# Retention's queries, keys and values as products of 512 columns in a hybrid decoder trunk

## The chip, the core and the metric

The kernel runs on one core of a Trainium2 chip. Its time is the device time of one execution in microseconds (us). Five engines work side by side, each in the order of its own queue: TensorE (PE, with its weight loads as PEld), VectorE (DVE), ScalarE (ACT), GpSimd (POOL) and SyncE (SP, which here issues DMAs). They wait for each other at semaphores. Matrix products accumulate in PSUM banks of 128 x 512 fp32; everything else lies in SBUF, 128 partitions wide.

## The reference, cut to what matters

Two layers (DEPTH = 2), a sequence of 1024 tokens, width 1024, all in fp32. Each layer has three groups of heads that read one projection of the normalised input: sliding-window attention (a), retention (r) and gated linear attention (g).

```python
h = rms_norm(x, pre_gain) * (1.0 + scale) + shift
proj = h @ w_in
(aq, ak, av, ag, rq, rk, rv, rg, gq, gk, gv, gg, ga) = jnp.split(proj, IN_SPLITS, axis=-1)
...
rq = apply_rotary(rq.reshape(B, S, RET_HEADS, RET_DK), positions, ret_freq)
rk = apply_rotary(rk.reshape(B, S, RET_HEADS, RET_DK), positions, ret_freq)
r = retention(rq, rk, rv.reshape(B, S, RET_HEADS, RET_DV))
r_out = rms_norm(r).reshape(B, S, RET_W) * jax.nn.silu(rg)
...
y = jnp.concatenate([a_out, r_out, g_out], axis=-1) @ w_out
return x + gate * rms_norm(y, post_gain)
```

Rotation turns the two halves x1, x2 (32 columns each) of every head's 64 columns into x1 cos - x2 sin and x2 cos + x1 sin. Retention runs over 8 chunks of 128 tokens with 4 heads of 64 columns: in each chunk the masked scores of queries against keys times the values, plus the queries times a state that is carried on from chunk to chunk; the state is a sum of decayed key-value products:

```python
sc = jnp.einsum('bhid,bhjd->bhij', qi, ki) * dmask
intra = jnp.einsum('bhij,bhjv->bhiv', sc, vi)
inter = jnp.einsum('bhid,bhdv->bhiv', qi * q_decay, state)
new_state = chunk_decay * state + jnp.einsum('bhjd,bhjv->bhdv', ki * k_decay, vi)
```

Queries, keys, values and retention's gate rg are 256 columns each of w_in; so are gg (the gate of the g group, with 16 columns more) and the other units.

## The kernel before

**Tiles and products.** The sequence is cut into 8 tiles t of 128 tokens, 4 pairs p of tiles, 2 halves hf of 4 tiles. Every fp32 operand is held as a high and a low part. A product over the 1024 inner columns is three passes (high x high, low x high, high x low) over 8 blocks k of 128: 24 matmuls that accumulate in one bank (`accum`). `project` holds the tile's 128 tokens (h) as the stationary side and moves the weights, 256 columns; its result has tokens on partitions. `project_P` and `project_T` hold 128 columns of the weights and move the tokens: a pair's 256, or a half's 512 from two tiles of memory with `both`; the result is transposed, with head columns on partitions. There are three banks for such products (the names `mm`) and five for the small ones (`aux`).

**Retention before.** For each pair p: `ret_q` makes two products of 24 matmuls of 256 columns into the two halves of one bank, and VectorE turns them: four operations 32 x 512, which read one quarter of the partitions of the bank, multiply with the sine and write to the neighbouring quarter (two of them with a factor -1), one product with the cosine, one sum. Then follow the keys of two tiles and the values of two tiles, 24 matmuls of 256 columns each, each in a bank of its own. A key tile is rotated by `rotary` on VectorE (five operations); a value tile is scaled by one. `ret_core` is the step of a tile: two transposes of the rotated keys on TensorE, a copy to SBUF by ScalarE, the scores (TensorE), two masks (VectorE), the outputs and the state's update (TensorE), the state's sum and decay (VectorE), then the norm and the gate (`head_norm_gate`: square by ScalarE, sum by VectorE, power by POOL, two products by VectorE, transposes).

**Order of the work.** TensorE's order is written out by hand, through a model clock. Each `mult` moves the clock on; `job` hands in a generator such as `ret_core`, whose `yield` says how long the model waits until the next piece of it may be issued (the table `L` holds these numbers; `rc1` is the wait before the key transposes, a name with @1 holds for layer 1); `flag` and `await_flag` do the same for results that others wait for. `pump` is called after each few matmuls and issues all pieces that are due in between. For the other engines a scheduler sets the order.

**Weights.** They are loaded in units of 1024 x 256 by `load`: four DMAs of 256 KB on SP into staging buffers, then converted to high and low parts by VectorE, ScalarE and POOL into one of seven places (`PLACES`; 0 to 2 lie in one array, `arena_71` in the orders below, 3 to 6 in another, `arena_479`). A place is free when the products of the unit that it held are done. `PLACE` says which unit goes where (the number `_w` is 0 in layer 0 and 2 in layer 1). Before: rg 5, rq 6, rk `_w`, rv 5; rv therefore follows rg in the same place, and its load is called behind the last gate product. SP also carries the stores of finished gates (srS, sgS), of the sine tables (tabA), and the loads of modulation weights (ms).

## Time and profile before

| | us |
|---|---|
| median of 3 runs (lowest, highest) | 981.45 (981.32, 981.62) |
| profiled execution, its own time | 980.64 |
| its span, first to last instruction | 978.5 |
| TensorE busy | 958.2 (98%) |
| VectorE busy | 678.2 (69%) |
| ScalarE busy | 395.6 (40%) |
| POOL busy | 247.7 (25%) |

The profile is of one execution. A group's row gives the line, the engine, the operation, output and inputs with shapes, the count, then the busy time in us and the mean of one in ns, then the idle time of the engine ahead of these instructions and what ended it. A timeline's row gives the start and the duration in us, the instruction and how often it follows itself; a wait ahead of it stands in brackets. Matmuls overlap in the pipeline, so the time that one costs is the distance between starts and not its duration. The retention of layer 0 lies at about 95 to 180 us, that of layer 1 at about 562 to 662 us.

### The profile page before, as it was taken

How to read it: one execution, taken by the hardware profiler on the slowest of the kernel's cores; microseconds unless marked ns; L12 is line 12 of the kernel's file. 1: busy time of each engine (PE TensorE's matmuls, PEld its weight loads, DVE VectorE, ACT ScalarE, POOL GpSimd, SP SyncE). 2: the span in 40 equal slices, each digit the busy share in tenths (PEclk: the TensorE clock that was granted, in tenths of full speed). 3: DMA queues.
4: the chain of work that ended last, by engine and by line, in shares of the span. 5: the costliest groups of instructions: out<-in, count | busy, mean ns of one | idle time of the engine just before them, and what ended most of it. 6: DMA issues, size and time to landing. Idle time of an engine off the chain costs nothing.

```text
span 978.5 us, 19647 instructions
## 1 busy us (share of the span) xinstructions
PE 958.2 (98%) x7228; PEld 825.8 (84%) x7228; DVE 678.2 (69%) x1598; ACT 395.6 (40%) x1112; POOL 247.7 (25%) x311
## 2 busy tenths in 40 slices
PE   7999999999999999999999999999999999999996
PEld 5799999889998777778889999988999877777875
DVE  6586768678675877645696466785765577677885
ACT  4674102233323656623355420133333257664231
POOL 3431111323310425410133100123332034544000
PEclk9999999999999999999999999999999999999998
DMA  9856315443243345587564121342132434389783
GB/s 353 295 176 197 114 42 150 134 125 103 88 119 118 119 148 184 167 279 242 203 230 152 60 87 33 119 150 62 63 97 77 129 92 135 108 265 282 246 281 121
DMA packets 107532, 150.34 MB, mean 154 GB/s; under 512 B 11142, under 2 KB 58536, under 8 KB 106412
## 3 DMA queue, kind: packets, MB, share of 16 engines
q1 hardware_dynamic: 96140, 134.75, 43.8%
q10 hardware_dynamic: 11296, 14.34, 4.1%
q8 instruction: 57, 0.93, 0.4%
q14 instruction: 39, 0.32, 0.1%
HBM read 110.25 MB, written 36.70 MB: 150 GB/s over the span
## 4 chain that ended last, share of the span: by engine, by line
PE 89%; DVE 6%; DMA 1%; POOL 1%; issue 1%; ACT 1%; SPq 0%; POOLq 0%; DVEq 0%; ACTq 0%
PE mm L170 67%; PE aux L170 18%; PE aux L185 4%; POOL sm L606 1%; DMA ms<-in_w_mod_dram 1%; DMA t<-in_x_dram 0%; DVE t L1288 0%; DVE t L1290 0%; SPq L866 0%; PE mm L185 0%; DVE t L1179 0%; POOL mx L1211 0%; DVE acc L317 0%; DVE t L1099 0%; DVE t L1291 0%
## 5 line engine op out<-in xcount | busy, mean ns | idle before, releaser
L170 PE MATMUL mm<-arena,arena 128*128 128x256 f32 (+2 forms) x1824 | 298.2, 316 | 2.7 <-DVE arena L156 1.4
L170 PE MATMUL mm<-arena 128*128 128x256 f32 (+2 forms) x1728 | 284.7, 318 | 0.0
L170 PEld LDWEIGHTS mm<-arena,arena 128*128 128x128 f32 x1824 | 252.6, 189 | 28.0 <-issue 7.9
L170 PEld LDWEIGHTS mm<-arena 128*128 128x128 f32 x1728 | 240.3, 189 | 24.3 <-issue 4.2
L606 POOL TENSOR_TENSOR sm<-sm,mhalf 128x1 f32<-128x1 f32 (+1 forms) x64 | 57.7, 901 | 292.6 <-DVE sm L603 153.8
L170 PE MATMUL mm<-arena,mx 128*128 128x512 f32 (+1 forms) x564 | 130.9, 388 | 0.0
L170 PEld LDWEIGHTS mm<-arena,mx 128*128 128x128 f32 x564 | 101.5, 188 | 24.0 <-issue 2.3
L154 ACT ACTIVATE t<-aux 128x256 f32<-128x256 f32 (+2 forms) x124 | 52.4, 438 | 97.3 <-PE aux L185 84.6
L154 ACT ACTIVATE arena<-st 128x512 fp32r<-128x512 f32 x94 | 56.1, 628 | 49.4 <-PE mm L170 20.3
L498 POOL TENSOR_TENSOR arena<-st,arena 128x512 fp32r<-128x512 f32 x32 | 45.7, 1429 | 97.5 <-ACT arena L154 81.1
L1049 POOL TENSOR_TENSOR smx<-smx,sm 128x512 f32<-128x512 f32 x32 | 35.0, 1094 | 124.8 <-DVE sm L1048 110.6
L498 DVE TENSOR_TENSOR arena<-st,arena 128x512 fp32r<-128x512 f32 x76 | 59.2, 799 | 3.1 <-ACT arena L154 1.6
L1045 ACT ACTIVATE smx<-smx,sm 128x129 f32<-128x129 f32 x128 | 49.9, 392 | 27.5 <-DVE sm L1042 27.3
L317 DVE SCALAR_TENSOR_TENSOR acc<-ms,c_act,acc 128x512 f32<-128x512 f32 x60 | 45.0, 749 | 17.1 <-DMA ms<-in_w_mod_dram 16.6
L1093 ACT ACTIVATE t<-aux 128x256 f32<-128x256 f32 x32 | 12.3, 383 | 77.3 <-PE aux L170 73.8
L170 PEld LDWEIGHTS aux<-t,mx 32*128 32x128 f32 (+1 forms) x896 | 39.8, 187 | 3.8 <-issue 1.7
L170 PE MATMUL aux<-t,mx 32*128 32x32 f32 (+1 forms) x896 | 40.9, 272 | 0.0
L1040 DVE COPY_PREDICATED smx<-c_masks,aux 128x256 f32<-128x256 int32 x64 | 25.3, 446 | 17.9 <-ACT smx L154 14.5
L1395 DVE SCALAR_TENSOR_TENSOR t<-t,sm,t 128x512 f32<-128x512 f32 x32 | 24.2, 780 | 18.4 <-DMA t<-in_x_dram 12.3
L185 PE MATMUL aux<-c_early,t 128*128 128x128 f32 x186 | 33.8, 277 | 1.5 <-ACT t L1225 0.9
L170 PEld LDWEIGHTS aux<-kT,mx 64*128 64x128 f32 x384 | 24.6, 185 | 10.9 <-issue 7.1
L1098 DVE TENSOR_TENSOR t<-aux,sm 128x256 f32<-128x256 f32 x32 | 13.6, 424 | 27.4 <-POOL sm L606 27.4
(264 smaller groups left out, 1426.9 us busy)
## 6 DMA issues: line engine op xcount, KB each, us to landing
st<-in_w_in_dram SPq DMA_DIRECT2D x96, 256.0 KB, 3.8
ms<-in_w_mod_dram SPq DMA_DIRECT2D x64, 256.0 KB, 3.7
mx<-mixS SPq DMA_DIRECT2D x20, 512.0 KB, 5.6
st<-in_w_last_dram SPq DMA_DIRECT2D x36, 256.0 KB, 3.3
wm<-in_w_m_dram SPq DMA_DIRECT2D x8, 1024.0 KB, 16.7
mixS<-t SPq DMA_DIRECT2D x40, 128.0 KB, 2.1
t<-in_x_dram SPq DMA_DIRECT2D x18, 256.0 KB, 5.0
mixS<-t ACTq DMA_DIRECT2D x32, 128.0 KB, 2.1
```

Source lines behind the costliest of these rows:

```text
L154: A.activation(dst, src, AF.Copy)
L170: T.matmul(dst, lhsT, rhs, start=start, stop=stop)
L185: T.transpose(dst, src, idn)
L317: V.scalar_tensor_tensor(acc, wt, c_act[:, k:k + 1], acc, ALU.mult, ALU.add)
L498: e.tensor_tensor(lo, st, f(hi), ALU.subtract)
L606: G.tensor_tensor(r, r, mhalf[:, :w], ALU.pow)
L1040: V.copy_predicated(sv, curmask.unsqueeze(1).to_broadcast((P, 2, P)), pv[:, :, n // P - 1, :])
L1045: A.activation(sm[:, h, :], sm[:, h, :], AF.Exp, bias=mx[:, h:h + 1], accum_out=sums[:, h:h + 1])
L1049: eng("pn").tensor_tensor(sm[:, :, 0:128], sm[:, :, 0:128], rs.unsqueeze(2).to_broadcast((P, 4, P)), ALU.mult)
L1093: A.activation(sq, po, AF.Square)
L1098: V.tensor_tensor(h4(g1), h4(po), r.unsqueeze(2).to_broadcast((P, 4, 64)), ALU.mult)
L1395: V.scalar_tensor_tensor(xt[j], yg[j], r, xt[j], ALU.mult, ALU.add)
```

## The change

**Queries.** `ret_q` now takes a half (four tiles): two products of 24 matmuls of 512 columns (`project_T`), each in a bank of its own. ScalarE copies the four quarters of the bank's partitions crosswise, with the factor 1 or -1, into SBUF; VectorE multiplies the bank with the cosine and the copies with the sine, and adds. All four of these products (two halves) stand ahead of all keys and values. The turned queries lie in two tiles, one for each half.

**Keys and values.** The new `project_2` holds the tile's tokens and moves the 256 columns of rk and the 256 columns of rv together: one product of 24 matmuls of 512 columns per tile, one bank. Columns 0 to 255 are rotated, columns 256 to 511 are scaled, and the tile's step is handed in at once; `rc1` goes from 0.8 (layer 0) and 0.0 (layer 1) to 4.0.

**Places and loads.** Both units must lie in the same array, rk in 5 and rv in 6; rg is in 6, rq in `_w`. rk is loaded first (layer 0: behind the first rg pair; layer 1: at the end of layer 0), rq behind the last gg product, rv behind the last rg product, gqk behind the last query product, gv and kv behind the last key-value product. The places of the attention weights and of the last layer's output weights are changed with that, and so are the points at which ag1, o2 and o3 are loaded.

**Gate order.** Layer 0: rg0, rg1, gg2, gg3, rg2, rg3 (before: gg3 behind rg2). Layer 1: gg0 to gg2, rg0, rg1, gg3, rg2, rg3 (before: all of rg0 to rg2 ahead of gg3).

TensorE's order in layer 0, from the last gate product on. Before (`mm_1197`, its last 17: the first queries; `mm_1311`, `mm_1350`: keys of tiles 0 and 1; `mm_1391`, `mm_1421`: values):

```order
L170 MATMUL mm_1197<-arena_71,arena_479 128x256 x17
L170 MATMUL mm_1311<-arena_71 128x256 x7
L185 MATMUL aux_1319<-c_early,ga_1115 48x128
L170 MATMUL mm_1311<-arena_71 128x256 x17
L170 MATMUL mm_1350<-arena_71 128x256 x24
L170 MATMUL mm_1391<-arena_479,arena_71 128x256 x24
L170 MATMUL mm_1421<-arena_479,arena_71 128x256 x14
```

The first value product stands 96 matmuls of 256 columns behind the last gate product. After (`mm_1172`: the last gate product; `mm_1254` to `mm_1389`: all queries; `mm_1426`, `mm_1469`: keys and values of tiles 0 and 1):

```order
L170 MATMUL mm_1172<-arena_479 128x256 x17
L185 MATMUL aux_1244<-c_early,ga_1046 48x128
L170 MATMUL mm_1254<-arena_71 128x512 x24
L170 MATMUL mm_1299<-arena_71 128x512 x12
L170 MATMUL aux_1317<-gaT_579,gwt 128x512
L170 MATMUL mm_1299<-arena_71 128x512 x12
L170 MATMUL mm_1352<-arena_479,arena_71 128x512 x24
L170 MATMUL mm_1389<-arena_479,arena_71 128x512 x24
```

Now 96 matmuls of 512 columns stand between the last gate product and the first product that reads the values' weights.

TensorE's order in layer 1, at the first tiles. Before (`mm_7131`: keys of tile 1; `mm_7175`, `mm_7210`: values of tiles 0 and 1; `mm_7254`: the next queries; `aux_7205`, `aux_7249`: key transposes; `aux_7225`, `aux_7226`: scores):

```order
L170 MATMUL mm_7131<-arena_71,arena_479 128x256 x17
L170 MATMUL mm_7175<-arena_479 128x256 x24
L185 MATMUL aux_7205<-c_early,t_1243_7124 128x128 x2
L170 MATMUL mm_7210<-arena_479 128x256 x14
L170 MATMUL aux_7225<-rq_7086,t_1254_7208 128x128
L170 MATMUL aux_7226<-rq_7086,t_1254_7208 128x128
L170 MATMUL aux_7225<-rq_7086,t_1254_7208 128x128
L170 MATMUL aux_7226<-rq_7086,t_1254_7208 128x128
L170 MATMUL mm_7210<-arena_479 128x256 x10
L185 MATMUL aux_7249<-c_early,t_1248_7166 128x128 x2
L170 MATMUL mm_7254<-arena_479 128x256 x14
```

Between the end of a key product and its transposes stand other tiles' key and value products. After (`mm_6878`: the last queries; `mm_6915`, `mm_6958`, `mm_7011`: keys and values of tiles 0, 1 and 2; `aux_6990`, `aux_7039`: key transposes; `aux_7018`, `aux_7019`: scores):

```order
L170 MATMUL mm_6878<-arena_71 128x512 x24
L170 MATMUL mm_6915<-arena_479 128x512 x24
L170 MATMUL mm_6958<-arena_479 128x512 x20
L185 MATMUL aux_6990<-c_early,t_1256_6949 128x128 x2
L170 MATMUL mm_6958<-arena_479 128x512 x4
L170 MATMUL mm_7011<-arena_479 128x512 x4
L170 MATMUL aux_7018<-rq_6699,t_1263_6993 128x128
L170 MATMUL aux_7019<-rq_6699,t_1263_6993 128x128
L170 MATMUL aux_7018<-rq_6699,t_1263_6993 128x128
L170 MATMUL aux_7019<-rq_6699,t_1263_6993 128x128
L170 MATMUL mm_7011<-arena_479 128x512 x12
L185 MATMUL aux_7039<-c_early,t_1265_7002 128x128 x2
```

Now 20 matmuls of 512 columns stand between a tile's product and its transposes.

VectorE's order in layer 1. Before, at the second pair's queries (`mm_7542`: queries; L1288, L1290, L1291, L1295: the turn; L1099 and L1086: the norm's last steps of an earlier tile; L944 to L949: the rotation of a key tile `mm_7659`):

```order
L1288 SCALAR_TENSOR_TENSOR t_1331_7651<-mm_7542,tab 32x512
L1099 TENSOR_TENSOR t_1329_7644<-t_1329_7644,t_1325_7635 128x256
L1290 TENSOR_TENSOR t_1331_7651<-mm_7542,tab 32x512
L1288 SCALAR_TENSOR_TENSOR t_1331_7651<-mm_7542,tab 32x512
L1291 TENSOR_TENSOR t_1330_7650<-mm_7542,tab 128x512
L331 TENSOR_TENSOR modg_6993<-aux_7681,ms_7683 128x512
L1295 TENSOR_TENSOR rq_7657<-t_1330_7650,t_1331_7651 128x512
L1086 TENSOR_TENSOR t_1339_7693<-aux_7686,t_1338_7692 128x256
L944 TENSOR_TENSOR t_1340_7701<-mm_7659,sincos 128x256
L946 TENSOR_TENSOR tr_7702<-mm_7659,sincos 128x4x32
L947 TENSOR_TENSOR tr_7702<-mm_7659,sincos 128x4x32
L948 TENSOR_TENSOR t_1340_7701<-t_1340_7701,tr_7702 128x4x32
```

The turn of the queries stands between the norm of one tile and the rotation of the next. After, at the last queries and the first keys (L1287 to L1289: what is left of the turn; L947 to L952: the rotation; L1644: the values):

```order
L1287 TENSOR_TENSOR t_1249_6906<-mm_6878,tab 128x512
L1288 TENSOR_TENSOR t_1250_6907<-t_1250_6907,tab 128x512
L1289 TENSOR_TENSOR rq_6828<-t_1249_6906,t_1250_6907 128x512
L947 TENSOR_TENSOR t_1256_6949<-mm_6915,sincos 128x256
L949 TENSOR_TENSOR tr_6950<-mm_6915,sincos 128x4x32
L950 TENSOR_TENSOR tr_6950<-mm_6915,sincos 128x4x32
L951 TENSOR_TENSOR t_1256_6949<-t_1256_6949,tr_6950 128x4x32
L952 TENSOR_TENSOR t_1256_6949<-t_1256_6949,tr_6950 128x4x32
L1644 TENSOR_TENSOR t_1258_6956<-mm_6915,c_late 128x256
L947 TENSOR_TENSOR t_1265_7002<-mm_6958,sincos 128x256
```

The queries' three operations stand ahead of the first tile's rotation, and a tile's rotation and value scaling follow each other.

The diff (the table L is cut to the two numbers that change):

```diff
 PLAIN = 2
-SW = dict(W00=6, T1=3, W11=4, W10=5, T2=2, T3=0, T4=1)
+SW = dict(W00=5, T1=3, W11=4, W10=6, T2=2, T3=0, T4=1)
 TOK = ((1, 2, 3, 4), (3, 4, 0, 1))
...
 for _t, _w in zip(TOK, (0, 2)):
-    PLACE.append(dict(gg=_w, rg=5, rq=6, rk=_w, rv=5, gqk=6, gv=_w, kv=5, aq0=6, aq1=_w, ag0=5, ag1=_w,
+    PLACE.append(dict(gg=_w, rg=6, rk=5, rq=_w, rv=6, gqk=_w, gv=5, kv=6, aq0=_w, aq1=5, ag0=6, ag1=_w,
                       o0=_t[0], o1=_t[1], o2=5, o3=6))
...
 
-    def project_P(pm, l, p, w, c):
-        h = hT[(l, p)]
-        accum(pm, lambda a, k: w[:, a, k, c:c + P], lambda b, k: h[:, b, k, 0:256])
+    def project_2(pm, l, t, w0, w1):
+        await_flag(("hT", l, t))
+        c = slice((t % 2) * P, (t % 2) * P + P)
+        h = hT[(l, t // 2)]
+        accum(pm.rearrange("p (s n) -> p s n", s=2), lambda a, k: h[:, a, k, c],
+              lambda b, k: both(w0[:, b, k, 0:256], w1[:, b, k, 0:256]))
 
...
 
-    def ret_q(l, p, w):
-        pm = mm()
+    def ret_q(l, hf, w):
+        rqT[hf] = gp.tile([P, NT * P], F32, tag=f"kT{hf}", name=nm("rq"), bufs=1)
+        sn, cs = (tab[:, i, 512 * hf:512 * hf + 512] for i in range(2))
         for c in range(2):
-            project_P(pm[:, 256 * c:256 * c + 256], l, p, w, c * P)
-
-        def two(x):
-            return x.rearrange("p (c n) -> p c n", c=2)
-
-        sn, cs = (tab[:, i, 256 * p:256 * p + 256].unsqueeze(1).to_broadcast((P, 2, 256)) for i in range(2))
-        u, x = t2(), t2()
-        for b in range(4):
-            r = slice(32 * b, 32 * b + 32)
-            o = two(x)[32 * (b ^ 1):32 * (b ^ 1) + 32]
-            if b % 2:
-                V.scalar_tensor_tensor(o, two(pm)[r], -1.0, sn[r], ALU.mult, ALU.mult)
-            else:
-                V.tensor_tensor(o, two(pm)[r], sn[r], ALU.mult)
-        V.tensor_tensor(two(u), two(pm), cs, ALU.mult)
-        if p % 2 == 0:
-            rqT[0] = gp.tile([P, NT * P], F32, tag=f"kT{p // 2}", name=nm("rq"), bufs=1)
-        q = rqT[0][:, 512 * (p % 2):512 * (p % 2) + 512]
-        V.tensor_tensor(q, u, x, ALU.add)
-        flag(("rq", l, p), L["rq1"])
-        return two(q)
-
-    rqT = [None]
+            pm = mm()
+            project_T(pm, l, hf, w, c * P)
+            u, x = t2(), t2()
+            for b in range(4):
+                r, o = (slice(32 * i, 32 * i + 32) for i in (b, b ^ 1))
+                A.activation(x[o], pm[r], AF.Copy, scale=-1.0 if b % 2 else 1.0)
+            V.tensor_tensor(u, pm, cs, ALU.mult)
+            V.tensor_tensor(x, x, sn, ALU.mult)
+            V.tensor_tensor(rqT[hf][:, 512 * c:512 * c + 512], u, x, ALU.add)
+            pump()
+        for p in (2 * hf, 2 * hf + 1):
+            flag(("rq", l, p), L["rq1"])
+
+    rqT = [None, None]
 
...
 
-    def ret_core(l, t, q, k, v):
+    def ret_core(l, t, k, v):
         yield lat("rc1", l)
...
         yield (0.0, ("rq", l, t // 2))
-        qT = q[:, :, P * (t % 2):P * (t % 2) + P]
+        qT = rqT[t // 4].rearrange("p (c n) -> p c n", c=2)[:, :, P * (t % 4):P * (t % 4) + P]
         yield lat("rc2", l)
...
             if p == NP_ - 1:
-                load(l, "rk" if name == "gg" else "rv")
+                load(l, "rq" if name == "gg" else "rv")
             if name == "gg" and p % 2:
...
         if l == 0:
-            for name, p in (("rg", 0), ("rg", 1), ("gg", 2), ("rg", 2), ("gg", 3), ("rg", 3)):
+            for name, p in (("rg", 0), ("rg", 1), ("gg", 2), ("gg", 3), ("rg", 2), ("rg", 3)):
                 do_gates(name, p)
                 if name == "rg" and p == 0:
-                    load(l, "rq")
+                    load(l, "rk")
         else:
-            for ps_ in ((0, 1, 2), (3,)):
-                for name in ("gg", "rg"):
-                    for p in ps_:
-                        do_gates(name, p)
+            for name, ps_ in (("gg", (0, 1, 2)), ("rg", (0, 1)), ("gg", (3,)), ("rg", (2, 3))):
+                for p in ps_:
+                    do_gates(name, p)
 
...
         await_flag("tab")
-        for p in range(NP_):
-            last = p == NP_ - 1
-            q = ret_q(l, p, used(l, "rq"))
+        for hf in range(2):
+            ret_q(l, hf, used(l, "rq"))
+        load(l, "gqk")
+        for t in range(NT):
+            pm = mm()
+            project_2(pm, l, t, used(l, "rk"), used(l, "rv"))
+            k = ret_k(t, pm[:, 0:256])
+            v = t1()
+            V.tensor_tensor(h4(v), h4(pm[:, 256:512]), vdec.unsqueeze(2).to_broadcast((P, 4, 64)), ALU.mult)
+            job(ret_core(l, t, k, v))
             pump()
-            if last:
-                load(l, "gqk")
-            ks = {}
-            for name in ("rk", "rv"):
-                w = used(l, name)
-                for tt in range(2):
-                    t = 2 * p + tt
-                    pm = mm()
-                    project(pm[:, 0:256], l, t, w)
-                    src = pm[:, 0:256]
-                    if name == "rv":
-                        v = t1()
-                        V.tensor_tensor(h4(v), h4(src), vdec.unsqueeze(2).to_broadcast((P, 4, 64)), ALU.mult)
-                        job(ret_core(l, t, q, ks[tt], v))
-                    else:
-                        ks[tt] = ret_k(t, src)
-                    pump()
-                if last:
-                    load(l, {"rk": "gv", "rv": "kv"}[name])
+        load(l, "gv")
+        load(l, "kv")
         G.memset(stC, 0.0)
...
                 if hf:
-                    if l == DEPTH - 1 and g == 0:
+                    if l == DEPTH - 1 and g:
                         sw_first("W00")
                     else:
-                        load(l, ("o3", "ag1")[g])
+                        load(l, ("ag1", "o2")[g])
         for hf in range(2):
...
                     else:
-                        load(l, "o2")
+                        load(l, "o3")
             if not hf:
...
         load(l + 1, "rg")
-        load(l + 1, "rq")
+        load(l + 1, "rk")
 
...
-     "rc1": 0.8,
-     "rc1@1": 0.0,
+     "rc1": 4.0,
+     "rc1@1": 4.0,
...
```

2 lines of the change are left out of this document (1 added, 1 removed).

## The prediction

> **What bounds the kernel now.** I read the page's busy table, the chain that ended last, and the row of the core, in this order.
>
> ```profile
> span 978.5 us, 19647 instructions
> PE 958.2 (98%) x7228; PEld 825.8 (84%) x7228; DVE 678.2 (69%) x1598; ACT 395.6 (40%) x1112; POOL 247.7 (25%) x311
> PE 89%; DVE 6%; DMA 1%; POOL 1%; issue 1%; ACT 1%; SPq 0%; POOLq 0%; DVEq 0%; ACTq 0%
> core 0: 978.5 us, clock 0.996
> ```
>
> TensorE is busy 98% of the span at nearly the full granted clock. So a change is worth what it takes out of TensorE's own stream, plus or minus the moments in which that stream stands still. The groups by shape, TensorE only, then single rows of its timeline (start, duration, count):
>
> ```profile
> L170 PE MATMUL mm<-arena,arena 128*128 128x256 f32 x1152 | 150.6, 285 | 2.7 <-DVE arena L156 1.4 <-DVE t L1291 1.3
> L170 PE MATMUL mm<-arena 128*128 128x256 f32 x1152 | 150.1, 285 | 0.0
> L170 PE MATMUL mm<-arena,arena 128*128 128x512 f32 x480 | 122.3, 402 | 0.0
> L170 PE MATMUL mm<-arena 128*128 128x512 f32 x480 | 122.1, 401 | 0.0
> ...
> 556.16 5.91 PE L170 MATMUL mm<-arena,arena 128*128 128x256 f32 x48
> 561.91 5.32 PE L170 MATMUL mm<-arena 128*128 128x256 f32 x43
> ...
> 296.39 9.43 PE L170 MATMUL mm<-arena 128*128 128x512 f32 x40
> 305.74 0.89 PE L170 MATMUL aux<-kT,mx 64*128 64x128 f32 x12
> ...
> 443.08 13.24 PE L170 MATMUL mm<-arena,mx 128*128 128x512 f32 x56
> 456.16 0.60 PE L185 MATMUL aux<-c_early,t 128*128 128x128 f32 x4
> ```
>
> The mean of 285 ns is one matmul's own length; they overlap. What counts is the distance from start to start: 256 columns (561.91 - 556.16) / 48 = 119.8 ns; 512 columns (305.74 - 296.39) / 40 = 233.8 ns, and (456.16 - 443.08) / 56 = 233.6 ns where the moving side comes from two weight slots (the output products). Twice the columns cost 5.9 ns less than twice the time. Busy time per instruction says the same: 150.1 / 1152 = 130.3, 122.1 / 480 = 254.4, so 6.2 ns per pair.
>
> The first row also holds the only waits of that shape, 2.7 us. Here they are, with what ended them:
>
> ```profile
> 101.43 4.80 PE L170 MATMUL mm<-arena,arena 128*128 128x256 f32 x38 [1.42 <-DVE arena L156]
> 645.10 1.07 PE L170 MATMUL mm<-arena,arena 128*128 128x256 f32 x7 [1.29 <-DVE t L1291]
> ...
> 87.50 2.13 SPq L159 DMA_DIRECT2D srS<-t x2
> 89.68 1.87 SPq L159 DMA_DIRECT2D st<-in_w_in_dram x4
> ...
> 100.88 0.41 DVE L156 CAST arena<-st 128x512 fp32r<-128x512 f32 x1
> ...
> 644.26 0.69 DVE L1291 TENSOR_TENSOR t<-mm,tab 128x512 f32<-128x512 f32 x1
> ```
>
> At 101.43 the first value product waits for its weights: their loads stand on SP's queue behind two stores of gates, go out at 89.68, and VectorE converts the first piece at 100.88. At 645.10 a product waits for its accumulator bank, which VectorE's late query arithmetic still reads.
>
> **The change, part by part.** (1) Fewer, wider matmuls. Per layer the queries go from 192 matmuls of 256 columns to 96 of 512, keys and values from 384 to 192; in both layers 576 pairs become 576 singles. At 5.9 to 6.2 ns a pair: 3.4 to 3.6 us; I take 3.5. The queries' form is that of the row at 296.39, the keys' and values' that of 443.08, so the bounds are narrow: 3.3 to 3.8.
>
> (2) The wait at 101.43 goes. The value weights are still loaded behind the last gate product, but are now first needed after all queries: 4 x 24 x 0.2337 = 22.4 us, where 101.43 - 1.42 - 89.68 = 10.3 us were to be had before. That is -1.4. The query weights come next in line: loaded behind the last gg product, with four rg products in front of the first query, 4 x 24 x 0.1198 = 11.5 us. The value weights took 11.6 us from issue at 89.68 to the first converted piece (100.88 + 0.41), with VectorE busy in between: cover equals need, so 0 to 1 us may come back here. The key weights go out much earlier (layer 0 behind the first rg pair, layer 1 in the layer before).
>
> (3) The wait at 645.10 goes: -1.3. While queries run no retention step competes, and TensorE needs 5.6 us for each bank, so with three banks a reader may be 11 us late.
>
> (4) Queries off VectorE. The stage's groups on VectorE (window 567.6 to 661), and the rows nearest to the new ScalarE copy:
>
> ```profile
> 567.60:661.00 93.40, 92.11 (x764) 88.34 (x763) 66.90 (x168) 19.12 (x43) 11.77 (x11) 1.00 0.29 90
> ...
> L1288 DVE SCALAR_TENSOR_TENSOR t<-mm,tab 32x512 f32<-32x512 f32 x8 | 5.5, 689 | 0.2
> L1290 DVE TENSOR_TENSOR t<-mm,tab 32x512 f32<-32x512 f32 x8 | 5.5, 685 | 0.2
> L1291 DVE TENSOR_TENSOR t<-mm,tab 128x512 f32<-128x512 f32 x4 | 2.8, 692 | 0.1
> L1295 DVE TENSOR_TENSOR rq<-t,t 128x512 f32<-128x512 f32 x4 | 2.7, 682 | 0.0
> ...
> L1359 ACT ACTIVATE t<-mm 128x512 f32<-128x512 f32 x15 | 8.9, 595 | 6.1 <-PE mm L170 6.0
> L972 ACT ACTIVATE va<-mm 128x128 f32<-128x128 f32 x16 | 4.4, 276 | 13.1 <-PE mm L170 10.8 <-ACT t L154 1.2 <-PE aux L185 0.6
> ```
>
> VectorE loses 12 of 24 query operations a layer, 16.5 to about 8.2 us. ScalarE gains 16 copies of 32x512 a layer. No row has that shape; between 276 (128 columns) and 595 ns (512 columns, from the same banks) I take 595, because VectorE's 32 and 128 partitions of 512 columns cost alike (685, 692), so columns set the time. That is 4 x 0.6 = 2.4 us a product on an engine that is busy 19 of 93 us, then about 2 us on VectorE; 4.4 is under the 5.6 us that a product takes. Cost on the path: 0. If ScalarE stands in a wait of its own, the banks' 11 us cover it.
>
> (5) Keys and values at once. A tile now brings rotation, value scaling and a retention step after one product of 5.6 us, instead of four products per pair. Rows of this stage (VectorE), then the small products on TensorE:
>
> ```profile
> L1326 DVE TENSOR_TENSOR t<-aux,c_late 128x256 f32<-128x256 f32 x16 | 6.0, 418 | 4.0 <-PE aux L170 3.8
> L317 DVE SCALAR_TENSOR_TENSOR acc<-ms,c_act,acc 128x512 f32<-128x512 f32 x8 | 6.0, 746 | 3.1 <-DMA ms<-in_w_mod_dram 3.1
> L944 DVE TENSOR_TENSOR t<-mm,sincos 128x256 f32<-128x256 f32 x8 | 3.3, 415 | 0.1
> L948 DVE TENSOR_TENSOR t<-t,tr 128x128 f32<-128x128 f32 x8 | 3.2, 399 | 0.0
> L949 DVE TENSOR_TENSOR t<-t,tr 128x128 f32<-128x128 f32 x8 | 2.2, 280 | 0.0
> L1095 DVE TENSOR_REDUCE sm<-t 128x4 f32<-128x256 f32 x7 | 2.9, 416 | 7.9 <-ACT t L1093 7.9
> L1098 DVE TENSOR_TENSOR t<-aux,sm 128x256 f32<-128x256 f32 x6 | 2.5, 425 | 2.3 <-POOL sm L606 2.3
> L1099 DVE TENSOR_TENSOR t<-t,t 128x256 f32<-128x256 f32 x6 | 2.5, 425 | 0.1
> ...
> 578.39 0.71 PE L170 MATMUL aux<-rq,t 64*128 64x128 f32 x8
> 579.03 1.47 PE L170 MATMUL mm<-arena 128*128 128x256 f32 x10
> ...
> 588.34 0.38 PE L170 MATMUL aux<-stR,rq 128*128 128x128 f32 x2
> 590.04 0.60 PE L170 MATMUL mm<-arena 128*128 128x256 f32 x3
> ```
>
> A tile's turn on TensorE is 24 x 0.2337 + 0.64 (scores) + 1.70 (outputs and state) + 0.14 (transposes) = 8.1 us. VectorE's share is (66.9 - 16.5) / 8 = 6.3 us, and about 0.4 of waiting for the power on POOL: 83% of a turn, where 66.9 / 93.4 = 72% was before. In the new order 20 matmuls, 4.7 us, stand between a key product's end and its transposes in layer 1. The rotation takes 0.42 + 0.40 + 3 x 0.28 = 1.7 us (its two other products cost what L949 costs), so 3.0 us are left for what stands ahead of it on VectorE: two masks 0.84, and the norm 0.42 + 0.43 + 0.43 with 0.4 of waiting for POOL, 2.5 together. This usually fits, with 0.5 us to spare. A single L317 (0.75, after a DMA) in the wrong place does not. I allow 0.1 us per tile over 16 tiles, 1.5 us, bounds 0 and 4.
>
> (6) Moved weights. Of the later loads gv and kv now go out after the last key product: gv needs its place after 2 x 24 x 0.2337 = 11.2 us, against the 11.6 us of part (2): 0 to 0.5. Attention weights and output weights are moved by one place, each load still at least one whole product (48 x 0.2337 = 11 us) ahead; 0, and -0.5 to 0.5 as bounds. Gate order: gg3 now runs before rg2 in layer 0 and rg2 after gg3 in layer 1; the same products on TensorE. In layer 0 gg3's first matmuls come 5.8 us (2 x 24 x 0.1198) earlier than before against the last normalised tile: 0 to 0.5.
>
> Sum: -3.5 - 1.4 - 1.3 + 1.5 (keys) + 0.5 (weights and gates) = -4.2. The profiled execution took 980.64 us (span 978.5), 0.81 below the median of 981.45; so its span would be 974.3, and the runs 981.45 - 4.2 = 977.2.
>
> The fixed part of a matmul is where the notes speak against this size: the Trainium skill, "TensorE: Matmul & The Clock Gate", section "Back-to-back issue gap", gives N / 2.4 + 2.5 ns for a warm array, by which a pair would save 2.5 ns and part (1) 1.4 us instead of 3.5; the sum would be -2.1, 979.3. The trace has 119.8 and 233.6, a fixed part of about 6 ns, and decides. The same section's sustained 131 ns at N = 512 would make the gain many times larger; the 233.6 excludes it here.
>
> **Rivals.** (a) The waits only change their place: query weights late behind gg3 in both layers (up to 1.4 each, as at 101.43), gv late (up to 1.4). For it: cover and need are both 11 us. Against: the first key product, whose weights go out behind gg3 and have 96 matmuls of 256 columns as cover too (two rg products, the first queries), did not wait:
>
> ```profile
> 94.09 0.99 PE L170 MATMUL mm<-arena 128*128 128x256 f32 x7
> ```
>
> If they do come late, -4.2 + 3 = -1.2: 980.2, no change.
>
> (b) Slower: VectorE is late for the transposes of every tile. For it: 83% of each turn, and the chain product, rotation, transposes, scores, masks, outputs runs within two turns. Against: three banks let TensorE go on, and the hand-written order puts 4.7 us of products in front. Without the 1.5 the sum is -5.7; from (5.7 + 2.0) / 16 = 0.48 us per tile it is slower by over 0.2%; at 0.8 us per tile 12.8 - 5.7 = +7: 988.5.
>
> (c) The wide products save nothing (their start-to-start with retention's small products in between is 239.6): -0.7 in all, 980.7. Against: both 512-column rows above. (The page's 2.5 ns a pair lies between this and the forecast.)
>
> (d) All new waits stay at zero: -6.2, 975.2.
>
> **How the numbers follow.** A difference under 0.2%, 2.0 us, is no change for a measurement of this kernel. Forecast with its range 975.5 to 979.3: 0.50, (d) and somewhat better: 0.15, (a): 0.14, (c): 0.04, (b): 0.17. Faster takes forecast and (d), and a little of (a): 0.68; same: 0.15; slower 0.17. The range reaches from 974.2, under (d) by the upper bound of part (1) and of (6), to 983.0, beyond (a) and (c) into the beginning of (b).
>
> **What would show it.** Right: 576 matmuls of 512 columns in retention at 233.6 to 234; no wait before the first value product, none with L1288 or L1289; query copies near 0.6 us; TensorE's waits in retention under 1 us a layer. Wrong: rows of transposes or outputs (aux) that wait for VectorE's L952 or L1321 at tile after tile; the first query product with a wait for L156 or L498; copies on ScalarE near 1 us.

## The result, and the profile after

The changed kernel took 984.41 us (median; 979.65 to 989.80), the kernel before 981.31 us on the same chip (978.66 to 984.62). The ratio is 1.0032, 95% interval 1.0018 to 1.0047: slower by 0.3%, where 977.2 us, faster by 0.4%, was forecast. It lies 1.4 us above the range. Among the 12 executions of "gv and kv behind the copy, order kept" one disturbed one, of 5270 us, is left out of the numbers below.

The profiled execution of the changed kernel took 986.67 us, its span is 984.9. First the page's lines that answer to those shown of before (span, busy table, chain, core), and the row of the granted clock in 40 slices:

```profile
span 984.9 us, 18518 instructions
PE 961.8 (98%) x6652; PEld 801.7 (81%) x6652; DVE 667.6 (68%) x1574; ACT 414.6 (42%) x1144; POOL 247.2 (25%) x311
PEclk8999999989999999999999999999999999999999
PE 4%; DVE 2%; DMA 1%; SPq 0%; issue 0%; POOLq 0%; DVEq 0%; ACT 0%; ACTq 0%
core 0: 984.9 us, clock 0.989
```

There are 576 matmuls less (7228 to 6652), and yet TensorE is busy 3.6 us longer. The clock tells why: 0.989 instead of 0.996; two of its 40 slices stand at 8. The chain breaks off after 7% of the span here and says nothing about the middle. The page's groups by shape, then the queries' crosswise copies on ScalarE:

```profile
L170 PE MATMUL mm<-arena,arena 128*128 128x512 f32 x768 | 193.3, 401 | 0.0
L170 PE MATMUL mm<-arena 128*128 128x512 f32 x768 | 192.6, 399 | 0.0
L170 PE MATMUL mm<-arena,arena 128*128 128x256 f32 x576 | 77.8, 290 | 0.0
L170 PE MATMUL aux<-t,mx 32*128 32x32 f32 x768 | 26.6, 279 | 1.7 <-DVE mx L1244 1.7
L185 PE MATMUL aux<-c_early,t 128*128 128x128 f32 x184 | 32.1, 277 | 2.7 <-DVE t L639 1.2 <-ACT t L1228 0.8 <-DVE mx L1244 0.6
...
L1286 ACT ACTIVATE t<-mm 32x512 f32<-32x512 f32 x32 | 18.9, 590 | 5.7 <-PE mm L170 5.3
```

Each form has 288 matmuls of 512 columns more and 576 of 256 columns less, and these groups show 0.0 us of waiting, where the 256-column group of before had 2.7. A crosswise copy takes 590 ns. The transposes (L185) wait 2.7 us in the whole kernel, and the key rotation's lines are not among those that release them. TensorE's timeline shows the distances from start to start in layer 0: first the queries of the first half, then those of the second half with the first keys and values:

```profile
90.56 8.59 PE L170 MATMUL mm<-arena 128*128 128x512 f32 x36
98.98 0.39 PE L170 MATMUL aux<-gaT,gwt 128*128 128x512 f32 x1
...
101.99 21.27 PE L170 MATMUL mm<-arena,arena 128*128 128x512 f32 x92
123.09 0.38 PE L185 MATMUL aux<-c_early,t 128*128 128x128 f32 x2
```

(98.98 - 90.56) / 36 = 233.9 ns, (123.09 - 101.99) / 92 = 229.3 ns. So everything that the forecast says of the products themselves came in. I laid the same pieces of TensorE's work in both profiled executions side by side and took the difference of their times, after less before (the place is named by the time of the kernel before; up to it the changed kernel has 288 matmuls less in layer 0 and 576 less in layer 1, all else alike):

| place in the program | after less before, us | change since the row above |
|---|---|---|
| layer 0, 23 us after the start | +2.2 | half clock around 15 us: 10.2 us, before 3.4 |
| layer 0, 203 us, behind retention | -1.2 | -3.4 |
| layer 0, 206 us | -1.75 | -0.5 (before waits 0.47 us here) |
| layer 0, 215 us | +3.75 | +5.5 |
| layer 0, 492 us | +4.7 | +0.97 |
| between the layers, 520 us | +5.7 | +1.0 |
| layer 1, 696 us, behind retention | +5.0 | -0.7 |
| layer 1, 698 us | +5.5 | +0.5 (after waits 0.40 us here) |
| near the end, 943 us | +6.4 | +0.9 |

The first row is not the change's: the profiled executions below have 0, 3.4 or 10.2 us of half clock between 13 and 26 us, and the changed kernel itself 10.2 in this one and 0 in another. In layer 0 the change gained 3.4 us up to the end of retention (forecast there: half of 3.5, and 1.4). Then it lost 5.5 us at one place. In layer 1 retention gained 0.7 us although a new wait of 2.4 us lies in it; without that wait it is 3.1 (forecast there: half of 3.5, and 1.3). The places, on TensorE's timeline (the bracket is the wait and what ended it):

```profile
208.92 3.05 PE L170 MATMUL aux<-t,mx 32*128 32x32 f32 x47 [1.74 <-DVE mx L1244]
...
525.83 1.09 PE L185 MATMUL aux<-c_early,t 128*128 128x128 f32 x8 [0.96 <-DVE t L639]
...
664.62 0.79 PE L170 MATMUL aux<-rq,t 64*128 64x128 f32 x8 [2.38 <-ACT t L154]
...
935.15 3.02 PE L170 MATMUL mm<-arena,a 128*128 128x512 f32 x12 [1.00 <-DVE t L1450]
```

**207 us: gated linear attention (GLA) waits for its masks.** VectorE's timeline ahead of it:

```profile
198.38 0.68 DVE L331 TENSOR_TENSOR modg<-aux,ms 128x512 f32<-128x512 f32 x1
...
207.90 0.75 DVE L317 SCALAR_TENSOR_TENSOR acc<-ms,c_act,acc 128x512 f32<-128x512 f32 x1 [1.24 <-DMA ms<-in_w_mod_dram]
208.57 0.88 DVE L1244 COPY_PREDICATED mx<-c_masks,aux 128x128 f32<-128x128 int32 x4
```

The masks (L1244) stand behind sums for the next layer's modulation (L317), and these wait for their loads. On SP's queue:

```profile
199.10 9.91 SPq L159 DMA_DIRECT2D ms<-in_w_mod_dram  x8
```

What ends the wait of these loads is VectorE's L331, the last step of the modulation stage ahead of them, which is done at 199.06. In the kernel before L331 ends at 199.93, the first of these loads goes out at 199.96, and the same masks start at 207.24. So the loads go out 0.9 us earlier, and yet the masks come 1.3 us later: VectorE's order has seven of the modulation's products and sums (L315, L317) between L331 and the masks, where five stood before. TensorE came to this place 1.75 us earlier. By these numbers some 1.3 us were to spare before (1.75 + 1.3 - 1.74), so the gain alone would have waited about 0.4 us, and gain and later masks together wait 1.74 (estimates). That is only 1.74 of the 5.5 us. The rest is the clock (times, busy times of PE, PEld, DVE, ACT and POOL, then the granted clock, DMA share and GB/s):

```profile
204.00:209.00 5.00, 3.26 (x18) 2.38 (x15) 3.46 (x11) 2.54 (x9) 0.00 (x0) 1.00 0.74 222
209.00:212.50 3.50, 3.50 (x56) 3.48 (x56) 3.50 (x9) 0.23 (x2) 1.29 (x3) 0.59 0.65 182
212.50:216.50 4.00, 4.00 (x19) 3.96 (x19) 2.25 (x7) 0.45 (x4) 1.27 (x3) 0.51 0.16 57
```

Behind the wait TensorE runs at about half clock for 3.50 x (1 - 0.59) x 2 + 4.00 x (1 - 0.51) x 2 = 6.8 us. From 216.5 on it is full again. Half of the 6.8 us, 3.4, is lost: 1.74 + 3.4 = 5.1 of the 5.5.

**525 us: the next layer's rg weights.** rg now takes place 6, in which an output unit lay until late. Its conversions (L156 and L498) come when VectorE should finish the last tiles, and stand ahead of tile 7's (L614 to L639):

```profile
517.46 1.77 DVE L156 CAST arena<-st 128x512 fp32r<-128x512 f32 x1
519.15 1.27 DVE L498 TENSOR_TENSOR arena<-st,arena 128x512 fp32r<-128x512 f32 x2
...
525.29 0.89 DVE L639 TENSOR_SCALAR t<-t,sm 128x512 f32<-128x512 f32 x2 [0.66 <-POOL sm L609]
```

**662 us: kv stands ahead of the last key copy.** ScalarE's timeline:

```profile
648.64 1.67 ACT L154 ACTIVATE arena<-st 128x512 fp32r<-128x512 f32 x3 [4.44 <-PE mm L170]
...
658.67 0.63 ACT L154 ACTIVATE arena<-st 128x512 fp32r<-128x512 f32 x1 [5.40 <-DMA st<-in_w_in_dram]
660.06 0.63 ACT L154 ACTIVATE arena<-st 128x512 fp32r<-128x512 f32 x1 [0.76 <-DMA st<-in_w_in_dram]
662.52 0.63 ACT L154 ACTIVATE arena<-st 128x512 fp32r<-128x512 f32 x1 [1.83 <-DMA st<-in_w_in_dram]
...
664.18 0.38 ACT L154 ACTIVATE t<-aux 128x256 f32<-128x256 f32 x1 [0.21 <-ACT t L154]
```

The last row copies the last tile's turned keys, which its scores need. Each unit has three pieces that ScalarE converts, and gv is loaded ahead of kv. gv's three are converted in one go at 648.64, as soon as the place is free; the three that wait for DMAs ahead of the copy are kv's (the run with gv's pieces on POOL shows it). The transposes that the last row copies from were done at 660.4.

### The profile page after: what moved, and what is told of

The parts are those of the page before. It is cut to its first block, busy times and chain, and to the rows that moved or that the text cites. A ratio compares the mean times of both kernels' runs of the same rounds, so it can differ in the third digit from the quotient of the medians.

```text
span 984.9 us, 18518 instructions
## 1 busy us (share of the span) xinstructions
PE 961.8 (98%) x6652; PEld 801.7 (81%) x6652; DVE 667.6 (68%) x1574; ACT 414.6 (42%) x1144; POOL 247.2 (25%) x311
## 5 line engine op out<-in xcount | busy, mean ns | idle before, releaser
L170 PE MATMUL mm<-arena,arena 128*128 128x512 f32 (+2 forms) x1536 | 296.2, 345 | 0.0
L170 PE MATMUL mm<-arena 128*128 128x512 f32 (+2 forms) x1440 | 279.8, 347 | 0.0
L170 PEld LDWEIGHTS mm<-arena,arena 128*128 128x128 f32 x1536 | 236.5, 190 | 36.9 <-issue 5.1
L170 PEld LDWEIGHTS mm<-arena 128*128 128x128 f32 x1440 | 223.0, 189 | 34.3 <-issue 3.5
L498 POOL TENSOR_TENSOR arena<-st,arena 128x512 fp32r<-128x512 f32 x32 | 45.4, 1420 | 121.5 <-ACT arena L154 102.2
L498 DVE TENSOR_TENSOR arena<-st,arena 128x512 fp32r<-128x512 f32 x76 | 62.8, 851 | 2.4 <-PE mm L170 1.7
L317 DVE SCALAR_TENSOR_TENSOR acc<-ms,c_act,acc 128x512 f32<-128x512 f32 x60 | 46.4, 773 | 11.7 <-DMA ms<-in_w_mod_dram 11.2
L185 PE MATMUL aux<-c_early,t 128*128 128x128 f32 x186 | 32.6, 276 | 2.7 <-DVE t L639 1.2
```

Of the source, the lines that this page charges most:

```text
L170: T.matmul(dst, lhsT, rhs, start=start, stop=stop)
L185: T.transpose(dst, src, idn)
L317: V.scalar_tensor_tensor(acc, wt, c_act[:, k:k + 1], acc, ALU.mult, ALU.add)
L498: e.tensor_tensor(lo, st, f(hi), ALU.subtract)
```

## The experiments

The theory after this reading: the products save what was forecast, and the gain is given back at these three late points, each a short instruction behind work that waits for a load; a half clock behind a wait doubles or triples its price. Its rivals: the change costs something everywhere (VectorE, ScalarE or the memory of the wide products), or any earlier TensorE would lose its time at the next load anyhow, so that a removed wait appears elsewhere.

Experiments that start from the changed kernel give their edit against it; "before" was run again beside each batch (medians 981.6, 981.3, 982.1 and 982.0 us).

**The changed kernel again.** No edit.

> The changed kernel once more, as it stands. Theory W (late points: the wider products save what was forecast, and four new waits of TensorE with a clock drop behind the first of them take it back): the trace shows the same waits again, about 1.7 us before the second group of small GLA products in layer 0 (near 207), 1.0 us at the last tile's transposes between the layers (near 525), 2.4 us before the last tile's scores in layer 1 (near 662); mean clock 0.989 to 0.994; time 984.4 within 1.5. Theory C (clock: the denser stream of 512 columns draws a lower clock by itself): half-clock stretches stand inside the retention's products, not behind a wait. Theory N (chance): the waits stand elsewhere or are gone, and the time is within 0.1% of the kernel before.

984.84 us, ratio 1.0041 (1.0019 to 1.0063). The waits are there again: 1.97 us for the masks, 2.31 for the last key copy. This time both have the half clock behind them; rows of TensorE's timeline, then windows from the wait at 204 and around that at 659:

```profile
205.84 2.17 PE L170 MATMUL aux<-t,mx 32*128 32x32 f32 x47 [1.97 <-DVE mx L1244]
661.51 1.30 PE L170 MATMUL aux<-rq,t 64*128 64x128 f32 x8 [2.31 <-ACT t L154]
...
204.00:213.00 9.00, 7.16 (x76) 7.09 (x77) 7.54 (x18) 1.34 (x6) 2.50 (x5) 0.70 0.50 159
661.00:665.00 4.00, 3.49 (x14) 2.83 (x15) 2.59 (x7) 1.04 (x3) 1.40 (x2) 0.57 0.68 225
```

So the waits belong to the kernel; whether the clock falls behind one of about 2 us differs from execution to execution. In both executions retention's products run at full clock up to the wait for the last key copy; a lower clock that the denser stream drew by itself would show there.

**The modulation later.** The next layer's modulation is handed in behind another flag, and its first three staging tiles wait for a state that is written later:

```diff
                 wt = mod_stage()
+                if (l, j, hh) == (1, 1, 0) and k < BMOD:
+                    V.tensor_copy(wt[:, 0:1], stC[:, 0:1])
                 dma("lwm", wt, w_mod[l, j, hh, :, k, :])
...
-            job(mod_all(l + 1, (1, 0), ("mod", l, 2)))
+            job(mod_all(l + 1, (1, 0), ("stG", l, 2)))
```

> The changed kernel with the next layer's modulation started later in layer 0 (its first three loads depend on the GLA state after tile 1), so that VectorE's masks of the first GLA pair no longer stand behind modulation sums that wait for their loads. Theory W: the wait near 207 falls from 1.7 to under 0.5 us and with it the half-clock stretch behind it; mean clock 0.994 to 0.997; 984.4 - 1.7 - 1.7 to 3.4 = 979.3 to 981.0. Theory C: the wait goes, the clock stays at 0.989 to 0.993; 982.7. If the late modulation sums only move the wait to another mask: 984.

989.04 us, 1.0054 (1.0029 to 1.0078). The wait at 207 and the half clock behind it are gone, as the first row shows, but the whole modulation with its loads now stands elsewhere, and new waits came: 0.67, 0.62, 0.84, 0.95, 1.12 and 1.87 us at 225, 244, 380, 409, 506 and 523 us; the second row is the first of them. The time lies above everything that was expected.

```profile
204.83 1.54 PE L170 MATMUL aux<-t,mx 32*128 32x32 f32 x48
225.27 1.41 PE L170 MATMUL aux<-t,mx 32*128 32x32 f32 x41 [0.67 <-DVE t L1091]
```

The place is confirmed, the remedy is not: moving the whole stage shows the rival's mechanism.

**The last key copy by VectorE.**

```diff
-            copy("rT", kTt, pt[:, 0:256])
+            if t == NT - 1:
+                V.tensor_copy(kTt, pt[:, 0:256])
+            else:
+                copy("rT", kTt, pt[:, 0:256])
```

> The changed kernel with one copy per layer moved: the transposed keys of the last tile are copied by VectorE instead of ScalarE, whose queue holds three weight conversions that wait for their loads in front of it. Theory W: the wait of 2.4 us before the last tile's scores in layer 1 falls under 0.7 us, all else stays: 984.4 - 1.9 = 982.5. Rival: VectorE's own queue has five operations of the same weights there (3.1 us), the copy comes just as late: wait 2 to 3 us, 984.4.

987.75 us, 1.0053 (1.0033 to 1.0074). The wait grew from 2.4 to 5.1 us. TensorE's row, then VectorE's queue ahead of the copy (L1309): behind conversions and a state update stands a norm, which waits for ScalarE and POOL.

```profile
663.44 1.23 PE L170 MATMUL aux<-rq,t 64*128 64x128 f32 x8 [5.08 <-DVE t L1309]
...
659.33 0.42 DVE L1098 TENSOR_REDUCE sm<-t 128x4 f32<-128x256 f32 x1 [1.34 <-ACT t L1096]
661.84 0.42 DVE L1101 TENSOR_TENSOR t<-aux,sm 128x256 f32<-128x256 f32 x1 [1.12 <-POOL sm L609]
662.97 0.41 DVE L1309 COPY t<-aux 128x256 f32<-128x256 f32 x1
```

So it is what stands ahead in the queue that counts, and VectorE's queue is worse here than ScalarE's, by more than the rival had it (2 to 3 us).

**rg's place back.** Places 5 and 6 are exchanged among the units, and the loads of o2 and o3 with them, as before:

```diff
-    PLACE.append(dict(gg=_w, rg=6, rk=5, rq=_w, rv=6, gqk=_w, gv=5, kv=6, aq0=_w, aq1=5, ag0=6, ag1=_w,
+    PLACE.append(dict(gg=_w, rg=5, rk=6, rq=_w, rv=5, gqk=_w, gv=6, kv=5, aq0=_w, aq1=6, ag0=5, ag1=_w,
...
-                        load(l, ("ag1", "o2")[g])
+                        load(l, ("ag1", "o3")[g])
```

> The changed kernel with places 5 and 6 exchanged in all units but the output weights', so that the next layer's rg again takes the place of the output unit that is done first. Theory W: the conversions of rg no longer hold up the last tile's sums on VectorE, the wait of 1.0 us at the last tile's transposes between the layers falls to 0 to 0.3: 984.4 - 0.8 = 983.6. Rival: the last tile is late because its chain of sums, power and scaling is late anyway (the earlier gates), wait 0.8 to 1.1, 984.4.

983.47 us, 1.0011 (0.9997 to 1.0026). The wait between the layers is gone (the row has no bracket); the others stay (1.25 us for the masks, 1.98 for the last key copy).

```profile
520.50 1.09 PE L185 MATMUL aux<-c_early,t 128*128 128x128 f32 x8
```

This point is shown: the exchange of places makes that wait. In time it is 1.4 us beside the changed kernel's 984.84 of the same batch, with intervals that overlap.

**The queries alone.** The kernel before, with the queries' part of the change (`ret_q` by halves, ScalarE's copies, all queries first) and nothing else.

> The kernel before with the queries' part of the change alone: two halves ahead of all keys, products of 512 columns, crosswise copies by ScalarE; keys, values, places, loads, gate order and the two waits of the table as before. Theory W: -1.2 us (192 pairs at 6 ns) and both waits of the kernel before gone (-2.7), so TensorE reaches layer 0's GLA about 3 us earlier, and there the masks behind the modulation sums take 1.5 to 2 us back, at times with a half-clock stretch of 3.4; no wait at the end of layer 1's retention: 978.5 to 981.5. Rival (the loss comes from keys and values in one product, nothing else): 977.7, no wait near 205.

981.2 us, 1.0000 (0.9981 to 1.0018). Both waits of before (101.43 and 645.10) are gone, and 192 pairs became single matmuls: 192 x 6 ns + 2.7 = 3.9 us should have come in. In its profiled execution waits of 0.48 us at 205 and 0.54 at 225 are new, and 1.85 near the end, just ahead of 930.89, with half clock behind it (the 0.69 of the window):

```profile
930.00:934.00 4.00, 3.11 (x9) 2.47 (x10) 3.15 (x6) 1.92 (x5) 0.00 (x0) 0.69 1.01 361
```

Here too the gain does not reach the end. The interval of 1.8 us to each side leaves open how much of it does.

**Keys and values alone.** The changed kernel with the queries by pairs and between the tiles again.

> The changed kernel with the queries by pairs again, as before (256 columns, turned by VectorE), each pair ahead of its two tiles; keys and values stay one product of 512 columns, places, loads and gate order as changed. Theory W: the values' weights are now needed after one pair of queries, 5.8 us, and take about 11 from the last gate product: a wait of 4 to 6 us in each layer; 384 pairs save 2.4; the late points stay: 988 to 993. Rival: the weights come within 6 us, no wait over 2: 983 to 985.

991.47 us, in a single execution. The value weights (rv), needed at once here, come 5.45 us late, and the eight matmuls behind it run at half clock:

```profile
102.39 3.78 PE L170 MATMUL mm<-arena,arena 128*128 128x512 f32 x8 [5.45 <-DVE arena L156]
102.30:105.70 3.40, 3.31 (x8) 2.64 (x9) 3.33 (x6) 0.00 (x0) 0.00 (x0) 0.50 0.25 82
```

So the two parts are not a sum: the queries in front are what gives the value weights their time.

**gv's pieces by POOL.**

```diff
                     A.activation(hi, st, AF.Copy)
+                elif name == "gv" and kc:
+                    G.tensor_copy(hi, st)
```

> The changed kernel with one thing moved: the three high parts of gv's weights that ScalarE converts are converted by POOL, so ScalarE's queue holds no load ahead of the last tile's keys. Theory W: the wait of 2.4 us before the last tile's scores in layer 1 falls under 0.7, the half-clock stretch behind it is gone; 984.6 - 1.8 to 3.4 = 981.2 to 982.8. Rival: the keys' transposes or VectorE's rotation are late anyway, wait 1.5 to 2.5: 984.6.

985.79 us, 1.0047 (1.0031 to 1.0062), above both expectations. The wait did not go (3.14 us). POOL now converts gv's three pieces in one go, where ScalarE did at 648.64 in the changed kernel; the three conversions that wait for loads ahead of the key copy are still there, at 655.95, 657.61 and 660.53. They are kv's, and this run moved the wrong unit:

```profile
645.92 1.94 POOL L496 CAST arena<-st 128x512 fp32r<-128x512 f32 x3 [3.69 <-PE mm L170]
...
662.62 1.29 PE L170 MATMUL aux<-rq,t 64*128 64x128 f32 x8 [3.14 <-ACT t L154]
...
660.53 0.63 ACT L154 ACTIVATE arena<-st 128x512 fp32r<-128x512 f32 x1 [2.29 <-DMA st<-in_w_in_dram]
```

**Places, loads and order together.** x3's places; gv and kv loaded behind the first gqk product, gv's loads made to follow the last key copy, and the second gqk group ahead of the first gv product:

```diff
+            if name == "gv" and kc:
+                A.activation(st[:, 0, 0:1], lastk[0][:, 0:1], AF.Copy)
             dma("lw", st, sv[:, 2 * kc:2 * kc + 2, :])
...
-        load(l, "gv")
-        load(l, "kv")
         G.memset(stC, 0.0)
...
         do_gqk(0, 0)
+        load(l, "gv")
+        load(l, "kv")
         do_gqk(0, 1)
-        do_gv(0)
         do_gqk(1, 0)
-        do_gv(1)
+        do_gv(0)
         do_gqk(1, 1)
+        do_gv(1)
```

> The changed kernel with all late points treated: places as in the run with rg's place exchanged; gv and kv loaded behind the first GLA query product, gv's loads only after the last tile's keys are copied; GLA's third query-key product ahead of the first gv product, so that gv has 16.8 us of cover and GLA's masks come 5.6 us later against the modulation loads. Theory W: no wait over 0.7 us in either retention or at the first GLA pair, none between the layers, mean clock 0.995 to 0.998: 981.5 - 3.5 - 2.7 + 1.5 = 976.8, range 975.5 to 979.5. Rival C (the clock falls by itself with the denser stream): waits gone, clock 0.990: 980.5. Rival M (VectorE's and the loads' pace is what counts in layer 0, a gain ahead of it is only waited for further on): waits of 1 to 2 us at later GLA or attention steps, 980 to 983.

988.64 us, 1.0075 (1.0047 to 1.0102), above everything that was expected. The treated waits are gone or under 0.9 us; new ones came with the other order of GLA, the two longest with half clock behind them:

```profile
310.87 0.33 PE L170 MATMUL aux<-kT,mx 64*128 64x128 f32 x2 [1.95 <-ACT mx L964]
728.81 0.45 PE L185 MATMUL aux<-c_early,t 128*128 128x128 f32 x1 [1.62 <-DVE t L954]
```

The rival held: three waits were removed at the price of more. Whoever changes the order of products moves waits; the next two runs therefore keep the order.

**gv and kv behind the copy, order kept.** x3's places; the load calls behind the first gqk product; ScalarE's conversions of gv's and kv's pieces 1 to 3 made to follow the last key copy:

```diff
                 else:
+                    if name in ("gv", "kv") and kc:
+                        A.activation(hi[:, 0, 0:1], lastk[0][:, 0:1], AF.Copy)
                     copy(f"whi{kc}", hi, st)
...
-        load(l, "gv")
-        load(l, "kv")
         G.memset(stC, 0.0)
...
         do_gqk(0, 0)
+        load(l, "gv")
+        load(l, "kv")
```

> Places as in the run with rg's place exchanged, and ScalarE's conversions of gv and kv made to follow the copy of the last tile's keys (their loads may start as before; one written column per piece sets the order); GLA's order stays as in the changed kernel. Theory W: no wait of 0.7 us or more between the layers or before the last tile's scores; the wait of 1.4 to 2.1 near 207 stays with its half-clock stretch: 983.5 - 2.1 (- 1.7 where the half-clock stretch behind it goes too) = 979.7 to 981.4. Rival M (time gained ahead of VectorE's and the loads' pace is waited for further on): the wait before the last scores goes, others of 1 to 2 us appear in layer 1's GLA or attention: 982.5 to 984.

982.1 us, ratio 0.9999 (0.9975 to 1.0023), between what the theory (up to 981.4) and its rival (from 982.5) expected. The waits ahead of the last scores and between the layers are both gone. A wait of 1.50 us at 202 stays, one group of small products earlier than in the changed kernel: it ends with VectorE's L1091, which stands behind modulation sums that wait for their loads. In this execution the clock is full behind it.

**And the masks.** The same, and the fourth of the modulation loads that stood in the way waits for the masks of GLA's first chunk:

```diff
                 wt = mod_stage()
+                if (l, j, hh, k) == (1, 1, 0, 3):
+                    V.tensor_copy(wt[:, 0:1], lasts[0][:, 0:1])
                 dma("lwm", wt, w_mod[l, j, hh, :, k, :])
...
+            if (l, p, c) == (0, 0, 0):
+                lasts[0] = f(scz[:, c, 3, :])
```

> The same, and the fourth and later modulation loads of the next layer's first part follow the masks of the first GLA pair's first chunk, so that VectorE no longer stands in three modulation sums ahead of these masks. Theory W: the wait near 207 falls under 0.7 us and the half-clock stretch behind it goes: 976.5 to 979.0, mean clock 0.995 to 0.998. Rival M: other waits of 1 us and more in the GLA or attention of layer 0, 980 to 983.

977.96 us against 982.12 before: ratio 0.9957, 0.9938 to 0.9975. This version beats both kernels. TensorE's three places, without a bracket:

```profile
204.10 1.54 PE L170 MATMUL aux<-t,mx 32*128 32x32 f32 x48
516.82 1.09 PE L185 MATMUL aux<-c_early,t 128*128 128x128 f32 x8
653.10 0.72 PE L170 MATMUL aux<-rq,t 64*128 64x128 f32 x8
```

Behind the first 20 us the longest wait left is 0.70 us, at 491 us. This execution (973.1 us, mean granted clock 0.998) shows full clock up to 700 us, at the start too, which by itself is worth some 1.7 us beside the profile of before (half of 3.4); so the verdict is the median of the runs, not this span. Over all 12 runs the mean granted clock is 0.9938, beside 0.9952 of the kernel before in the same batch: some loss of clock is left, and what it stands behind in the other executions is not shown.

**The masks alone, on the changed kernel and on the one before.** The masks' edit above, with nothing else, once on each.

> The changed kernel with the last step alone: the fourth and later modulation loads follow the first masks of GLA; places and the order of gv's and kv's conversions as in the changed kernel. Theory W: the wait near 207 and the half-clock stretch behind it go, those of 1.0 near 525 and 2.4 near 662 stay: 984.6 - 1.9 - 1.7 to 3.4 = 979.3 to 981.0, mean clock 0.993 to 0.997. Rival (the three treatments only work together): 983 to 985.

> The kernel before with the same step alone. It has no wait at the first masks but 0.5 us on another engine near 205. Theory W (the step only gives back what the change had lost there): no difference, ratio 0.999 to 1.001. Rival (the step is worth 2 to 4 us in any kernel, and the gain of the treated kernel is not the change's): 0.996 to 0.998.

On the changed kernel 981.28 us, 0.9996 (0.9981 to 1.0011), that is 3.1 us less than its 984.4 and 0.3 above what was expected. A wait of 1.1 us at the transposes just ahead of them took the place of the masks' 1.74, with full clock behind it:

```profile
204.38 0.44 PE L185 MATMUL aux<-c_early,t 128*128 128x128 f32 x2 [1.10 <-ACT t L1232]
...
200.00:209.00 9.00, 7.90 (x130) 6.50 (x132) 5.02 (x16) 2.88 (x10) 0.56 (x2) 1.00 0.28 75
```

On the kernel before 982.69 against 981.98, 1.0005 (0.9992 to 1.0019): nothing. So the edit is no speed-up of its own; it gives back what the change lost. With the 3.3 us of the other two points (981.28 to 977.96, from different batches, whose medians of before agree within 0.2 us) the gain of the last version is made up. The edit for gv's and kv's conversions was not tried on the kernel before.

## Why the prediction was wrong

Its mechanism was right, and its sum left out three late points and what the clock makes of them.

- **Part (1), fewer and wider matmuls, right.** 229 to 234 ns from start to start, against 233.6 to 234 forecast; 576 instructions less. The rival "wide products save nothing" (c) falls.
- **Parts (2) and (3), the two old waits, right.** No wide product waits; the query weights, the named risk of 0 to 1 us, were in time. In layer 0, with half of (1) and all of (2), 3.15 us were due, and 3.4 came in; in layer 1, with half of (1) and all of (3), 3.05 were due, and 3.1 came in beside the new wait.
- **Part (4), right.** 590 ns a copy against 600 forecast, and no wait for it.
- **Part (5), too careful.** 1.5 us were set aside for VectorE being late for the transposes of every tile. That did not happen (rival (b), 988.5 us): the transposes' 2.7 us lie between the layers and in GLA. The allowance was made for the wrong place.
- **Part (6), "moved weights", is the step that failed first.** gv and kv were priced at 0 to 0.5 us, by whether gv's own product would have its weights in time. It had. What was late is the key copy behind kv's conversions on ScalarE: 2.4 us. For kv no time was worked out. The exchange of places was priced at 0, between -0.5 and 0.5, since each load was a whole product ahead; for rg, of which no price was made, it meant conversions on VectorE at the layer's end: 1.0 us. In both the needed time of the moved weight was weighed, and not what their conversions stand in front of.
- **The masks were not in the sum at all.** 1.74 us. The prediction looked at the stage that it changed; the next stage's masks stand behind modulation sums and their loads, which moved by 0.9 us where TensorE moved by 1.75, and two more of these sums came to stand ahead of the masks.
- **No term for the clock.** The prediction treats a microsecond of waiting as a microsecond. Behind the wait at 207 the half clock cost 3.4 us more.

Made new with these terms: the gains of (1) to (3) are -6.2 (in the profile -3.4 - 3.1 = -6.5); the three waits 1.74 + 0.96 + 2.38 = 5.1; together with the 1.0 at the end -0.1. The mean granted clock was 0.9919 over the 20 runs after, and 0.9952 over the 98 runs of the kernel before beside the experiments; over the changed kernel's own 20 runs the time rises by 0.88 us for each 0.001 less, so 0.0033 make 2.9. The sum is +2.8, measured 3.1. This is an account that closes, not a proof of each term: the line through the runs is a correlation, the three points were shown by removing them, the 1.0 at the end was not, and the 0.97 us between 215 and 492 us is not in it; with it the sum would be 3.8. Rival (a), "the waits only change their place", came nearest in kind, but named query weights and gv, which were in time. The range's lower end of 974.2 is 0.2 us under what its terms add up to: 975.2 - 0.3 - 0.5 = 974.4.

That the forecast's 4.2 us and the last version's 4.2 us (982.12 - 977.96) are the same figure is partly chance, since that version adds edits of its own and has small waits left. It shows that a gain of this size was there to be had.

## What to carry to other kernels

When loads or conversions move, look not only at whether their own consumer gets them in time, but at each short instruction behind them in the queues of ScalarE and VectorE: a conversion that waits for a DMA holds up a copy of 0.4 us for 2 us. Time gained in one stage reaches the end only if the next stage's operands come with it; check the first places behind the change for work that is tied to a load's own time. On a TensorE that is busy 98% of the span, price a wait of 2 us at 2 to 5 us, and first remove such waits without changing the order of the products.

## What the runs showed of the hardware

**Half clock behind short waits.** In the fourteen profiled executions, between 30 and 960 us, the granted clock was at half in 16 stretches of 3.4 or 6.8 us. Each begins in a wait of TensorE or within 3 us behind it: eleven waits of 1.25 to 2.3 us, three of 3.1 to 5.5 us, and two of only 0.59 and 1.03 us. Behind nine others of 1.25 to 2.4 us, the two waits of the kernel before among them, the clock stayed full, and two executions of the changed kernel differ at the same wait, that for the last key copy. The Trainium skill, "TensorE: Matmul & The Clock Gate", section "The HAM clock gate", has a free-running window of 3.4 us: the stretches found here, 3.4 and 6.8 us, and the 10.2 us early in the run, agree with it. Its table lets the clock fall after an idle window of about 3.4 us; here a wait of 1.74 us sufficed, among small matmuls of 32x32, and once one of 0.59. Why it falls behind one such wait and not behind another stays open.

**A conversion can take four times as long.** L156 on 128x512 took 0.41 us in the kernel before (at 100.88) and 1.77 us at 517.46 of the changed one, while POOL was writing at the same time:

```profile
517.14 1.81 POOL L907 MEMSET mx<- 128x2048 f32 x1 [1.45 <-PE mm L170]
```

The conversion ended at 519.23, 0.28 us behind POOL's operation. That POOL is the cause is only argued, from this coincidence.

**Copies of a quarter of the partitions are not cheaper.** 590 ns for 32x512 on ScalarE, beside the 595 ns that 128x512 took before: the columns set the time.

**Left open:** the wait near 930 us, 0.2 to 1.9 us in every profiled execution but that of the kernel before; the 0.97 us between 215 and 492; and how much of the half clock at 13 to 26 us is in each median.
